# A four-layer hybrid trunk on one core: two-stream norms with their sums and products in PSUM, maps' slabs asked for two units ahead, the first norm's sums from the token tiles

## The chip, the cores and the metric

The kernel runs on one core of a Trainium2 chip, in one launch. The metric is the device time in microseconds (us). Three executions of the kernel before took 2185.64, 2183.06 and 2180.51 us, median 2183.06.

## The reference, cut to what matters

256 latent tokens (x) and 256 context tokens (ctx) of width 1024 go through four layers, in fp32: Hyena (long convolution), GLA (gated linear attention), MLA (latent attention), Hyena. Each layer has a mixer and an MLP, and ahead of both stands a norm that is modulated by six maps of the layer:

```python
mod_l = jnp.split((silu_c @ ada_w[i] + ada_b[i])[:, None, :], 6, axis=-1)      # ada_w[i]: 1024 x 6144
h_lat = modulate(rmsnorm(x_lat, norm1_g[i]), mod_l[0], mod_l[1])               # h * (1 + scale) + shift
x_lat = x_lat + mod_l[2] * mixer(h_lat)
x_lat = x_lat + mod_l[5] * sq_relu_mlp(modulate(rmsnorm(x_lat, norm2_g[i]), mod_l[3], mod_l[4]), w1, w2)
```

`rmsnorm` is y * rsqrt(mean(y*y) + 1e-6) * g. The context tokens take the same path with their own maps as long as a later layer reads them. So the norms of Hyena 0, its MLP, GLA, its MLP and MLA run on both streams (512 tokens); those of MLA's MLP and of layer 3 on the latent tokens alone.

## The kernel before, in words

The residual lies transposed: `xT[k]` (L324) holds features k*128 to k*128+127 of all 512 tokens, latent first. Every fp32 product is made of three fp32r matmuls (`mm3`, L368): both factors are split into a high part (fp32r) and the rest. Weights come as 512 KB slabs by SyncE's DMA queue (`wload`, L336); ScalarE (ACT) casts the high part `wh` (L359) and GpSimd (POOL) subtracts it for the low part `wl` (L360). There are 5 buffers of `wraw` and 4 each of `wh` and `wl`.

PSUM has eight banks, shared out by tag (L145): `mm` 2, `cv` 3, `ada` 1, `st` 2. `bank(tag)` (L149) takes one.

**The two-stream norm** (`norm_mod`, L515) runs `stream(0)` for the latent and `stream(1)` for the context tokens. For each stream `token_rstd` (L481) squares the eight feature tiles on ACT (L490; POOL in the very first norm, L488), adds them on VectorE (DVE) in SBUF (`sacc`, L497), sums over partitions on TensorE (PE) with ones (L501), and `rsqrt` (L470) makes exp(-0.5*ln(v)) on ACT (L474, L475) with one Newton step on DVE (L476 to L478). `token_diag` (L507) puts the result on a diagonal, on DVE (L510), and one matmul (L524) spreads it over the partitions as `rb`. Then, for each k:

```python
nc.vector.scalar_tensor_tensor(t, xT[k][:, s], sc, rb[:, :SEQ], ALU.mult, ALU.mult)      # L528, t in SBUF
nc.scalar.activation(uH[k][:, s], t, AF.Identity, bias=sh)                               # L529
nc.vector.scalar_tensor_tensor(uL[k][:, s], t, sh, rounded(uH[k][:, s]), ALU.add, ALU.subtract)   # L530
```

`stream(0)` is moved ahead of the second half of the residual product before it (`last_part`, L532). The first products behind a norm read the streams one after the other, so that they can start on the latent half. Behind an MLP's norm (`first_product`, L697) products 0 and 1 lie in `mm`, 2 and 3 in `cv`; behind Hyena 0's norm all three are in `mm` (L944); in GLA the gates' product is in `mm` (L175) and q and k of the first head in `cv` (L1193); MLA's q part is in `mm` (L1400), its key and value part in `cv` and `st`. The residual product before is in the other tag: mixers' in `mm`, MLPs' in `cv` (L646, L780).

**The one-stream norm** (`lone_norm`, L574) does the same for the latent tokens alone, behind its products; what it squares and splits (`fresh`) lies in PSUM, two features to a bank (L587, L588), and so does its running sum (L597). It shares `rsqrt` and `token_diag` (L610).

**The maps.** For layers 0 and 1, `ada_units` (L396) is a generator: one unit asks for one slab of `ada_w` (`adaw`, 3 buffers) and multiplies it on PE (L410). `pump(n, keep)` (L459) runs n units at set places: 16 up front, 8 among the filters, then 8 in step 0 and 4 in every other step of Hyena 0 (L1135), where `keep` 8 holds back the last map. Layer 1's units follow behind. The maps of layers 2 and 3 are made in GLA's MLP by `ada_lone` (L417): 96 units, each one slab (`lw`), summed on DVE (L434 to L442) in `st` banks; two of the maps need both streams. `more` (L758) lets a unit go each time that `total`/96 matmul counts have passed; `total` (L756) is 7*192-24 = 1320 for the MLP's eight groups.

The order on each engine is a planner's: instructions come in program order by priority, an engine takes the next one that is ready in the planner's own timing, and a tile waits for a free buffer of its tag. Tokens come in as eight tiles `xr` (L250), which PE transposes (L328) and DVE copies (L329). The start also makes the Hyena filters' input (L297 to L322).

Of the kernel before, what the change touches and what calls it, by code (L numbers as in the profile page):

```python
# [11 lines left out]
F32 = mybir.dt.float32  # L12
# [6 lines left out]
P = 128  # L19
# [108 lines left out]
def trunk_kernel(ctx: ExitStack, tc: tile.TileContext, ins: dict, table, zpos, out, layers=(0, 1, 2, 3)):  # L128
# [195 lines left out]
    xT = [cp.tile([P, TOK], F32, tag=f"x{k}", name=f"x{k}") for k in range(KD)]  # L324
    for k in range(KD):
        ps = bank("cv")
        for j in range(4):
            nc.tensor.transpose(ps[:, j * P : (j + 1) * P], xr[2 * j + k // 4][:, (k % 4) * P : (k % 4 + 1) * P], ident)  # L328
        nc.vector.tensor_copy(xT[k], ps)  # L329
# [38 lines left out]
    def mm3(ps, lh, ll, rh, rl, start, stop):  # L368
        nc.tensor.matmul(ps, lh, rh, start=start, stop=False)  # L369
        nc.tensor.matmul(ps, lh, rl, start=False, stop=False)  # L370
        nc.tensor.matmul(ps, ll, rh, start=False, stop=stop)  # L371
# [24 lines left out]
    def ada_units(i, parts, first=False):  # L396


        for q in parts:
            ps = bank("ada")  # L400
            for k in range(KD):
                tag, bufs = "adaw", 3
                if first and q < 2:
                    tag = (("adaw", "wraw", "wh", "wl") * 3 + ("wraw", "wh", "wl", "wraw"))[8 * q + k]
                    bufs = {"adaw": 3, "wraw": 5, "wh": 4, "wl": 4}[tag]
                wt = wp.tile([P, D], F32, tag=tag, name=nm("adaw"), bufs=bufs)
                nc.sync.dma_start(wt, g["ada_w"][i, k * P : (k + 1) * P, q * D : (q + 1) * D])
                wv = wt.rearrange("p (t j c) -> p j t c", j=4, c=32)
                for j in range(4):
                    nc.tensor.matmul(ps[32 * j : 32 * j + 32, :256], sT[:, k, :], wv[:, j],  # L410
                                     start=k == 0, stop=k == KD - 1, tile_position=(0, 32 * j))
                if k < KD - 1:
                    yield
            ada_part(i, q, ps[:, :256], slice(0, 2))
            yield
# [54 lines left out]
    def rsqrt(v, n):  # L470
# [5 lines left out]
        nc.vector.scalar_tensor_tensor(t, y, -0.5, y, ALU.mult, ALU.mult)  # L476
# [4 lines left out]
    def token_rstd(r, on_pool=False):  # L481

        s = slice(r * SEQ, (r + 1) * SEQ)
        acc = np_.tile([P, SEQ], F32, tag="sacc", name=nm("sacc"), bufs=1)

        def square(dst, k):
            if on_pool:
                nc.gpsimd.tensor_tensor(dst, xT[k][:, s], xT[k][:, s], ALU.mult)  # L488
            else:
                nc.scalar.activation(dst, xT[k][:, s], AF.Square)  # L490

        square(acc, 0)
        for k in range(1, KD):
            sq = np_.tile([P, SEQ], F32, tag="sq", name=nm("sq"))
            square(sq, k)
            if k < KD - 1:
                nc.vector.tensor_tensor(acc, acc, sq, ALU.add)  # L497
        ps = bank("st")
        for j in range(2):
            for e, a in enumerate((acc, sq)):  # L500
                nc.tensor.matmul(ps[:, 2 * j : 2 * j + 2], a[:, j * P : (j + 1) * P], ones[:, 0:2],  # L501
                                 start=e == 0, stop=e == 1)
        v = np_.tile([P, 2], F32, tag="rs_v", name=nm("rsv"))
        nc.vector.tensor_scalar(v, ps[:, 0:4:2], 1.0 / D, EPS, ALU.mult, ALU.add)
        return rsqrt(v, 2)
# [9 lines left out]
    def norm_mod(i, which, nt, first=False):  # L515
# [3 lines left out]
        uL = [up.tile([P, TOK], F32R, tag=f"uL{k}", name=nm("uL")) for k in range(KD)]  # L519
        def stream(r):  # L520
            s = slice(r * SEQ, (r + 1) * SEQ)
            y = token_rstd(r, first)
            rb = bank("st")
            nc.tensor.matmul(rb[:, :SEQ], ones, token_diag(y), start=True, stop=True)  # L524
            for k in range(KD):
                t = np_.tile([P, SEQ], F32, tag="xr", name=nm("xr"))
                sc, sh = a[:, which, k, r : r + 1], m[:, 3 * which, k, r : r + 1]
                nc.vector.scalar_tensor_tensor(t, xT[k][:, s], sc, rb[:, :SEQ], ALU.mult, ALU.mult)  # L528
# [45 lines left out]
    def lone_norm(i, which, mp):  # L574
# [27 lines left out]
        def statistics():  # L602
            ps = bank("st")
            for j in range(2):
                for e, a in enumerate((acc, sq)):
                    nc.tensor.matmul(ps[:, 2 * j : 2 * j + 2], a[:, j * P : (j + 1) * P], ones[:, 0:2],  # L606
                                     start=e == 0, stop=e == 1)
            v = np_.tile([P, 2], F32, tag="rs_v", name=nm("rsv"))
            nc.vector.tensor_scalar(v, ps[:, 0:4:2], 1.0 / D, EPS, ALU.mult, ALU.add)
            diag = token_diag(rsqrt(v, 2))  # L610
# [72 lines left out]
    def mlp(i, nt, later=None, lone=()):  # L683
        single = nt == SEQ
        if not single:
            u = norm_mod(i, 1, nt)
        with ExitStack() as es:
# [68 lines left out]
            total, count = (groups - 1) * (4 * 24 + 8 * 12) - 24, [0]  # L756
# [156 lines left out]
    def hyena(i, j, nt, build):  # L913

        two = nt == TOK
        if two:
            u = norm_mod(i, 0, nt, build)
# [4 lines left out]
        with tc.tile_pool(name=nm("hy"), bufs=2, reuse_waits="tile") as mp:  # L922
# [77 lines left out]
            with tc.tile_pool(name=nm("hc"), bufs=2, reuse_waits="tile") as mq:  # L1000
# [111 lines left out]
                for step in range(units + 1):  # L1112
# [22 lines left out]
                    pump(8 if step == 0 else 4, 8)  # L1135
# [18 lines left out]
    def gla(i, j):  # L1154
# [4 lines left out]
        u = norm_mod(i, 0, nt)  # L1159
# [212 lines left out]
    def mla(i, j):  # L1372
        nt = TOK
        QR, KVR = 384, 256
        u = norm_mod(i, 0, nt)
# [263 lines left out]
    y = token_rstd(0)  # L1639
# [39 lines left out]
```

## Time and profile before

| | |
|---|---|
| the profiled execution | 2186.09 us, its span 2184.3 us |
| median of three executions | 2183.06 us (2180.51 to 2185.64) |
| PE busy | 2071.4 us (95%) |
| DVE, ACT, POOL busy | 1276.7, 908.8, 1088.7 us |
| mean granted PE clock | 0.97 of 2.4 GHz |
| DMA | 329 MB, mean 151 GB/s |

Times in the views are us from the span's start. PE is busy almost throughout, so what a part of the kernel can give or take shows where PE stands idle or where its granted clock falls to the lower of its two levels (1.2 GHz, 0.5 of full speed). The other engines' busy shares say little: they work beside PE.

### The profile page before, as it was taken

What the parts mean: (1) busy time and instruction counts of PE and PEld (TensorE: products, weight loads), DVE (VectorE), ACT (ScalarE), POOL (GpSimd) and SP (SyncE); (2) the same over time, 40 slices, a digit from 0 to 9 for tenths busy, and PEclk for the clock granted to TensorE, in tenths of its full rate; (3) what the DMA queues carried; (4) which work ended last, traced back from release to release, by engine and by line L of the source; (5) the groups of instructions that cost most, each with busy time, mean ns of one, the idle gap of its engine ahead of it and who ended that gap; (6) DMA issues with size and microseconds to landing.
All of it is one profiled execution on the core that took longest, in us unless ns stands there. A gap on an engine that the chain in (4) does not pass through costs nothing. (4 is left out here: it accounts for less than half of the span.)

```text
span 2184.3 us, 33342 instructions
## 1 busy us (share of the span) xinstructions
PE 2071.4 (95%) x12882; PEld 1769.6 (81%) x12882; DVE 1276.7 (58%) x2378; ACT 908.8 (42%) x1529; POOL 1088.7 (50%) x637
## 2 busy tenths in 40 slices
PE   6998999889999999999989999998999998899998
PEld 3766687677888888887788778788789998888998
DVE  7864887765433335555466986677662224883323
ACT  2643343343333334555242223226454546554544
POOL 5663454346545433333134444434346887455885
PEclk7999999999999999999999999999999999999999
DMA  9676635533333332322127688753135665443663
GB/s 317 192 223 202 231 96 180 191 93 118 105 98 108 109 92 68 85 59 77 39 78 231 209 281 269 252 183 98 65 96 161 188 193 160 141 140 116 187 181 116
DMA packets 322301, 329.12 MB, mean 151 GB/s; under 512 B 21276, under 2 KB 248673, under 8 KB 322143
## 3 DMA queue, kind: packets, MB, share of 16 engines
q1 hardware_dynamic: 321012, 326.05, 48.1%
q8 instruction: 101, 1.65, 0.3%
q10 hardware_dynamic: 587, 0.61, 0.1%
q0 software_dynamic: 544, 0.34, 0.1%
q14 instruction: 57, 0.47, 0.1%
HBM read 317.51 MB, written 9.44 MB: 150 GB/s over the span
## 5 line engine op out<-in xcount | busy, mean ns | idle before, releaser
L360 POOL TENSOR_TENSOR wl<-wraw,wh 128x1024 fp32r<-128x1024 f32 (+2 forms) x378 | 908.5, 2418 | 894.0 <-ACT wh L359 838.9
L359 ACT CAST wh<-wraw 128x1024 fp32r<-128x1024 f32 (+2 forms) x378 | 390.7, 1042 | 624.6 <-PE mm L370 243.4
L369 PE MATMUL mm<-uH,wh 128*128 128x512 f32 (+3 forms) x1272 | 448.5, 356 | 18.2 <-ACT uH L587 6.7
L370 PE MATMUL mm<-uL,wh 128*128 128x512 f32 (+3 forms) x1272 | 449.7, 355 | 10.3 <-DVE uL L530 9.3
L371 PE MATMUL mm<-uH,wl 128*128 128x512 f32 (+3 forms) x1272 | 445.1, 352 | 0.0
L369 PEld LDWEIGHTS mm<-uH,wh 128*128 128x128 f32 (+1 forms) x1272 | 244.7, 194 | 62.4 <-issue 10.0
L370 PEld LDWEIGHTS mm<-uL,wh 128*128 128x128 f32 (+1 forms) x1272 | 246.2, 194 | 46.3 <-DVE uL L530 13.3
L371 PEld LDWEIGHTS mm<-uH,wl 128*128 128x128 f32 (+1 forms) x1272 | 246.7, 194 | 32.3 <-issue 3.8
L369 PE MATMUL cv<-fH,wh 128*128 128x512 f32 (+1 forms) x576 | 209.3, 369 | 7.1 <-ACT fH L176 6.0
L370 PE MATMUL cv<-fL,wh 128*128 128x512 f32 (+1 forms) x576 | 210.7, 367 | 0.7 <-DVE fL L177 0.6
L371 PE MATMUL cv<-fH,wl 128*128 128x512 f32 (+1 forms) x576 | 209.2, 366 | 0.0
L666 DVE SCALAR_TENSOR_TENSOR x<-cv,mods,x 128x256 f32<-128x256 f32 x256 | 112.3, 477 | 84.9 <-PE cv L371 84.9
L370 PE MATMUL sum<-fL,wh 128*128 128x256 f32 x512 | 138.8, 278 | 0.0
L369 PE MATMUL sum<-fH,wh 128*128 128x256 f32 x512 | 137.1, 278 | 0.0
L371 PE MATMUL sum<-fH,wl 128*128 128x256 f32 x512 | 136.7, 278 | 0.0
L369 PEld LDWEIGHTS cv<-fH,wh 128*128 128x128 f32 x576 | 108.1, 189 | 29.3 <-ACT fH L176 7.6
L370 PEld LDWEIGHTS cv<-fL,wh 128*128 128x128 f32 x576 | 108.6, 189 | 19.1 <-DVE fL L177 1.1
L718 DVE SCALAR_TENSOR_TENSOR mm<-mm,r 128x512 f32<-128x512 f32 x60 | 41.8, 696 | 139.1 <-ACT r L717 138.9
L371 PEld LDWEIGHTS cv<-fH,wl 128*128 128x128 f32 x576 | 108.6, 189 | 17.7 <-issue 0.2
L436 DVE SCALAR_TENSOR_TENSOR st<-lw,sT,st 128x512 f32<-128x512 f32 x144 | 101.2, 747 | 8.3 <-DMA lw<-in_ada_w_dram 8.2
L621 DVE COPY rbias<-st 128x1 f32<-128x1 f32 x32 | 5.1, 159 | 163.1 <-PE st L371 162.9
L370 PEld LDWEIGHTS sum<-fL,wh 128*128 128x128 f32 x512 | 95.2, 188 | 0.0
(526 smaller groups left out, 4498.1 us busy)
## 6 DMA issues: line engine op xcount, KB each, us to landing
wraw<-in_mlp_w_dram SPq DMA_DIRECT2D x256, 512.0 KB
adaw<-in_ada_w_dram SPq DMA_DIRECT2D x96, 512.0 KB
lw<-in_ada_w_dram SPq DMA_DIRECT2D x96, 512.0 KB
wraw<-in_hy_w_in_dram SPq DMA_DIRECT2D x48, 512.0 KB
wraw<-in_gla_w_in_dram SPq DMA_DIRECT2D x24, 512.0 KB
spec<-S SPq DMA_DIRECT2D x16, 512.0 KB
wraw<-in_hy_w_out_dram SPq DMA_DIRECT2D x16, 512.0 KB
S<-spec SPq DMA_DIRECT2D x32, 256.0 KB
```

Of the source, the lines that this page charges most:

```text
L359: nc.scalar.copy(wh[r0:r1, :n], raw[r0:r1, :n])
L360: nc.gpsimd.tensor_tensor(wl[r0:r1, :n], raw[r0:r1, :n], rounded(wh[r0:r1, :n]), ALU.subtract)
L369: nc.tensor.matmul(ps, lh, rh, start=start, stop=False)
L370: nc.tensor.matmul(ps, lh, rl, start=False, stop=False)
L371: nc.tensor.matmul(ps, ll, rh, start=False, stop=stop)
L436: nc.vector.scalar_tensor_tensor(dst, wt[:, cols], sT[:, k, 0:1], run[b], ALU.mult, ALU.add)
L621: nc.vector.tensor_copy(bias, ps[:, SEQ : SEQ + 1])
L666: add = nc.vector.scalar_tensor_tensor(xT[dt][:, q], ps[:, q], mods[i][:, gi, dt, r : r + 1], xT[dt][:, q], ALU.mult, ALU.add)
L718: nc.vector.scalar_tensor_tensor(r, r, 0.0, pos, ALU.max, ALU.mult)
```

## The change

- The first norm's mean squares come from the token tiles: eight ACT squares with an accumulated sum, for both streams, ahead of the transposes; half of the transposes' copies go to ACT. The POOL squares, the `sacc` sums and the L501 matmuls of that norm fall away.
- In all two-stream norms one `st` bank holds the running sum, the four token sums, two operands of `rsqrt` and then `rb`; `t` goes to PSUM, two features to a bank, in `mm` (mixers) or `cv` (MLPs). `rsqrt` gets one more Exp, into PSUM, and `token_diag` moves to ACT. The one-stream norms take over these last two.
- `ada_units` asks for the slab of unit n+2 in unit n, from the same three buffers. `pump` in Hyena 0 gives 4 units in step 0 and 2 in the others.
- `total` becomes 6*192 = 1152.

```diff
+    def transpose_in(k):
+        ps = bank("cv")
+        for j in range(4):
+            nc.tensor.transpose(ps[:, j * P : (j + 1) * P], xr[2 * j + k // 4][:, (k % 4) * P : (k % 4 + 1) * P], ident)
+        (nc.scalar.copy if k % 2 else nc.vector.tensor_copy)(xT[k], ps)
...
+    sums = cp.tile([P, 8], F32, tag="xsum", name="xsum")
+    junk = wp.tile([P, SLOT], F32, tag="wl", name="junk", bufs=4)
+    for b in range(8):
+        nc.scalar.activation(junk[:, :512], xr[b], AF.Square, accum_out=sums[:, b : b + 1])
+    means = cp.tile([P, 4], F32, tag="xmean", name="xmean")
+    nc.vector.tensor_tensor(means, sums[:, 0:8:2], sums[:, 1:8:2], ALU.add)
+    nc.vector.tensor_scalar(means, means, 1.0 / D, EPS, ALU.mult, ALU.add)
     for k in range(KD):
...
+        transpose_in(k)
...
     def ada_units(i, parts, first=False):
...
+        slabs = [(q, k) for q in parts for k in range(KD)]
+        loaded = {}
+
+        def load(n):
+            q, k = slabs[n]
+            tag, bufs = "adaw", 3
...
+            loaded[n] = wp.tile([P, D], F32, tag=tag, name=nm("adaw"), bufs=bufs)
+            nc.sync.dma_start(loaded[n], g["ada_w"][i, k * P : (k + 1) * P, q * D : (q + 1) * D])
+
+        for n, (q, k) in enumerate(slabs):
+
+            for ahead in range(n, min(n + 3, len(slabs))):
+                if ahead not in loaded:
+                    load(ahead)
+            if k == 0:
+                ps = bank("ada")
+            wv = loaded.pop(n).rearrange("p (t j c) -> p j t c", j=4, c=32)
+            for j in range(4):
+                nc.tensor.matmul(ps[32 * j : 32 * j + 32, :256], sT[:, k, :], wv[:, j],
+                                 start=k == 0, stop=k == KD - 1, tile_position=(0, 32 * j))
...
-    def rsqrt(v, n):
+    def rsqrt(v, n, ps=None):
...
         nc.scalar.activation(y, t, AF.Exp, scale=-0.5)
-        nc.vector.scalar_tensor_tensor(t, y, -0.5, y, ALU.mult, ALU.mult)
+        y2 = y
+        if ps is not None:
+            y2 = ps[:, :n]
+            nc.scalar.activation(y2, t, AF.Exp, scale=-0.5)
+            t = ps[:, n : 2 * n]
+        nc.vector.scalar_tensor_tensor(t, y2, -0.5, y, ALU.mult, ALU.mult)
...
-    def token_rstd(r, on_pool=False):
+    def token_rstd(r, ps):
...
+        run = ps[:, :SEQ]
         acc = np_.tile([P, SEQ], F32, tag="sacc", name=nm("sacc"), bufs=1)
...
+        for k in range(KD):
+            sq = np_.tile([P, SEQ], F32, tag="sq", name=nm("sq")) if k else None
+            nc.scalar.activation(sq if k else run, xT[k][:, s], AF.Square)
+            if 0 < k < KD - 1:
+                nc.vector.tensor_tensor(acc if k == KD - 2 else run, run, sq, ALU.add)
+        st = ps[:, SEQ : SEQ + 4]
...
+        return rsqrt(v, 2, ps[:, SEQ + 4 : SEQ + 8])
...
         for j in range(2):
-            nc.vector.tensor_scalar(diag[:, j], ident, y[:, j : j + 1], None, ALU.mult)
+            nc.scalar.activation(diag[:, j], ident, AF.Copy, scale=y[:, j : j + 1])
...
-    def norm_mod(i, which, nt, first=False):
+    def norm_mod(i, which, nt, tag, known=None):
...
-            y = token_rstd(r, first)
-            rb = bank("st")
-            nc.tensor.matmul(rb[:, :SEQ], ones, token_diag(y), start=True, stop=True)
+            ps = bank("st")
+            y = token_rstd(r, ps) if known is None else known[:, 2 * r : 2 * r + 2]
+            rb = ps[:, :SEQ]
+            nc.tensor.matmul(rb, ones, token_diag(y), start=True, stop=True)
             for k in range(KD):
-                t = np_.tile([P, SEQ], F32, tag="xr", name=nm("xr"))
+                if k % 2 == 0:
+                    t2 = bank(tag)
+                t = t2[:, k % 2 * SEQ : (k % 2 + 1) * SEQ]
...
-            total, count = (groups - 1) * (4 * 24 + 8 * 12) - 24, [0]
+            total, count = (groups - 2) * (4 * 24 + 8 * 12), [0]
...
-            u = norm_mod(i, 0, nt, build)
+            u = norm_mod(i, 0, nt, "mm", rsqrt(means, 4) if build else None)
...
-                    pump(8 if step == 0 else 4, 8)
+                    pump(4 if step == 0 else 2, 8)
```

The other calls pass `"mm"` (GLA, MLA) and `"cv"` (MLP); `statistics` in `lone_norm` (L602) passes four columns of its `st` bank to `rsqrt`, and the final norm a bank of its own.

## Rows read from the trace of the kernel before

**Rows 1.** The profile page: busy us, share of the span and instructions of the engines.

```profile
PE 2071.4 (95%) x12882; PEld 1769.6 (81%) x12882; DVE 1276.7 (58%) x2378; ACT 908.8 (42%) x1529; POOL 1088.7 (50%) x637
```

**Rows 2.** Windows: start:end and length, busy us by engine, granted clock, DMA share, GB/s.

```profile
36.00:60.00 24.00, 19.08 (x89) 12.85 (x82) 21.83 (x34) 11.72 (x21) 16.23 (x12) 0.57 1.03 303
175.00:195.00 20.00, 14.40 (x107) 8.90 (x97) 6.08 (x15) 4.05 (x7) 2.41 (x1) 0.74 0.88 298
400.00:412.00 12.00, 10.01 (x86) 6.88 (x85) 7.66 (x11) 3.19 (x5) 5.63 (x5) 0.86 0.83 299
428.00:460.00 32.00, 26.36 (x179) 23.55 (x179) 27.19 (x52) 14.26 (x31) 10.58 (x8) 0.95 0.26 78
833.00:848.00 15.00, 11.59 (x66) 10.41 (x65) 12.97 (x30) 7.70 (x17) 7.06 (x5) 0.77 0.49 137
1099.00:1118.00 19.00, 12.98 (x70) 12.31 (x69) 14.49 (x27) 7.24 (x15) 5.91 (x3) 0.73 0.33 110
1199.00:1264.00 65.00, 62.60 (x283) 49.65 (x282) 63.13 (x88) 15.38 (x19) 28.24 (x11) 0.97 0.68 212
1485.00:1500.00 15.00, 12.55 (x54) 11.02 (x54) 14.71 (x27) 8.61 (x18) 8.81 (x4) 0.77 0.46 131
```

**Rows 3.** PE's waits: what it waited for, us in total, times, longest.

```profile
PE ada L410 <- DMA adaw<-in_ada_w_dram: 11.3, 12, 2.9
PE mm L370 <- DVE uL L530: 9.3, 8, 2.1
PE st L501 <- DVE sacc L497: 5.5, 4, 2.9
```

**Rows 4.** Timeline of all engines from 1102.4 us: start, duration, instruction, idle before it.

```profile
1102.85 4.84 POOL L360 TENSOR_TENSOR wl<-wraw,wh 128x1024 fp32r<-128x1024 f32 x2 [2.79 <-ACT wh L359]
1103.12 2.37 DVE L497 TENSOR_TENSOR sacc<-sacc,sq 128x256 f32<-128x256 f32 x1
...
1105.42 2.56 DVE L530 SCALAR_TENSOR_TENSOR uL<-xr,mods,uH 128x256 fp32r<-128x256 f32 x1
1105.64 0.35 PE L501 MATMUL st<-ones,sacc 128*128 128x2 f32 x2 [1.48 <-DVE sacc L497]
...
1108.03 0.58 PE L370 MATMUL mm<-uL,wh 128*128 128x256 f32 x1 [2.03 <-DVE uL L530]
```

**Rows 5.** Single lines: duration in ns min/median/max, first and last start.

```profile
L530 DVE SCALAR_TENSOR_TENSOR uL<-xr,mods,uH x80: 466/484/3711, 40.1 to 1511.8; 128x256 fp32r<-128x256 f32 x80
...
L588 DVE SCALAR_TENSOR_TENSOR uL<-sum,adam,uH x24: 473/476/484, 1630.3 to 1987.6; 128x256 fp32r<-128x256 f32 x24
...
L497 DVE TENSOR_TENSOR sacc<-sacc,sq x66: 405/424/2372, 16.9 to 2175.5; 128x256 f32<-128x256 f32 x66
...
L597 DVE TENSOR_TENSOR mm<-mm,sq x15: 417/431/433, 1633.4 to 1988.7; 128x256 f32<-128x256 f32 x15
...
L528 DVE SCALAR_TENSOR_TENSOR xr<-x,adam,st x80: 461/473/482, 39.0 to 1509.8; 128x256 f32<-128x256 f32 x80
```

**Rows 6.** Single lines, the same columns: ACT's shares of a norm.

```profile
L475 ACT ACTIVATE rsy<-rst x20: 190/204/207, 31.5 to 2177.6; 128x2 f32<-128x2 f32 x15, 128x4 f32<-128x4 f32 x5
...
L587 ACT ACTIVATE uH<-sum,adam x24: 464/476/556, 1629.6 to 1987.0; 128x256 fp32r<-128x256 f32 x24
```

**Rows 7.** MLA's norm, timeline of all engines: its first product and its second.

```profile
1484.27 0.87 DVE L528 SCALAR_TENSOR_TENSOR xr<-x,adam,st 128x256 f32<-128x256 f32 x2
...
1485.34 0.44 PE L369 MATMUL mm<-wh,uH 128*128 128x384 f32 x1
...
1494.54 0.73 PE L369 MATMUL cv<-wh,uH 128*128 128x320 f32 x2
```

**Rows 8.** First norm, timeline of PE: the wait for the second sum, and the first product.

```profile
39.27 0.56 PE L501 MATMUL st<-ones,sacc 128*128 128x2 f32 x2 [2.92 <-DVE sacc L497]
...
45.05 0.58 PE L369 MATMUL mm<-uH,wh 128*128 128x256 f32 x1
```

**Rows 9.** What ACT's L587 waited for in the one-stream norms: us, times.

```profile
  DVE uL L588: 1.4, 4
```

More of the change, by code (lines that the diff above doesn't have):

```diff
@@ L324, in trunk_kernel @@
     xT = [cp.tile([P, TOK], F32, tag=f"x{k}", name=f"x{k}") for k in range(KD)]
+    sums = cp.tile([P, 8], F32, tag="xsum", name="xsum")
[5 more added lines that the diff above has]
+    nc.vector.tensor_scalar(means, means, 1.0 / D, EPS, ALU.mult, ALU.add)
     for k in range(KD):
[L326 to L329, printed above, removed]
+        transpose_in(k)
     pre = nc.scalar.preload_act_table_set("natural_log_exp_and_others")
@@ L370, in mm3 @@
         nc.tensor.matmul(ps, lh, rl, start=False, stop=False)
-        nc.tensor.matmul(ps, ll, rh, start=False, stop=stop)
+        return nc.tensor.matmul(ps, ll, rh, start=False, stop=stop)
     mods = {}
@@ L396, in ada_units @@
     def ada_units(i, parts, first=False):
[L399 to L414, printed above, removed]
+        slabs = [(q, k) for q in parts for k in range(KD)]
[3 more added lines that the diff above has]
+            tag, bufs = "adaw", 3
+            if first and q < 2:
+                tag = (("adaw", "wraw", "wh", "wl") * 3 + ("wraw", "wh", "wl", "wraw"))[8 * q + k]
+                bufs = {"adaw": 3, "wraw": 5, "wh": 4, "wl": 4}[tag]
+            loaded[n] = wp.tile([P, D], F32, tag=tag, name=nm("adaw"), bufs=bufs)
[10 more added lines that the diff above has]
+                                 start=k == 0, stop=k == KD - 1, tile_position=(0, 32 * j))
+            if k == KD - 1:
+                ada_part(i, q, ps[:, :256], slice(0, 2))
+            loaded[n] = None
             yield
@@ L479, in rsqrt @@
         return y
-    def token_rstd(r, on_pool=False):
+    def token_rstd(r, ps):
         s = slice(r * SEQ, (r + 1) * SEQ)
+        run = ps[:, :SEQ]
         acc = np_.tile([P, SEQ], F32, tag="sacc", name=nm("sacc"), bufs=1)
[L486 to L498, printed above, removed]
+        for k in range(KD):
[4 more added lines that the diff above has]
+        st = ps[:, SEQ : SEQ + 4]
         for j in range(2):
             for e, a in enumerate((acc, sq)):
-                nc.tensor.matmul(ps[:, 2 * j : 2 * j + 2], a[:, j * P : (j + 1) * P], ones[:, 0:2],
+                nc.tensor.matmul(st[:, 2 * j : 2 * j + 2], a[:, j * P : (j + 1) * P], ones[:, 0:2],
                                  start=e == 0, stop=e == 1)
         v = np_.tile([P, 2], F32, tag="rs_v", name=nm("rsv"))
-        nc.vector.tensor_scalar(v, ps[:, 0:4:2], 1.0 / D, EPS, ALU.mult, ALU.add)
-        return rsqrt(v, 2)
+        nc.vector.tensor_scalar(v, st[:, 0:4:2], 1.0 / D, EPS, ALU.mult, ALU.add)
+        return rsqrt(v, 2, ps[:, SEQ + 4 : SEQ + 8])
     def token_diag(y):
@@ L603, in statistics @@
             ps = bank("st")
+            st = ps[:, SEQ : SEQ + 4]
             for j in range(2):
                 for e, a in enumerate((acc, sq)):
-                    nc.tensor.matmul(ps[:, 2 * j : 2 * j + 2], a[:, j * P : (j + 1) * P], ones[:, 0:2],
+                    nc.tensor.matmul(st[:, 2 * j : 2 * j + 2], a[:, j * P : (j + 1) * P], ones[:, 0:2],
                                      start=e == 0, stop=e == 1)
             v = np_.tile([P, 2], F32, tag="rs_v", name=nm("rsv"))
-            nc.vector.tensor_scalar(v, ps[:, 0:4:2], 1.0 / D, EPS, ALU.mult, ALU.add)
-            diag = token_diag(rsqrt(v, 2))
+            nc.vector.tensor_scalar(v, st[:, 0:4:2], 1.0 / D, EPS, ALU.mult, ALU.add)
+            diag = token_diag(rsqrt(v, 2, ps[:, SEQ + 4 : SEQ + 8]))
             def rstd():
@@ L1638, in trunk_kernel @@
         transposed(k)
-    y = token_rstd(0)
+    y = token_rstd(0, bank("st"))
     transposed(KD - 1)
```

8 lines of the change are left out of this document (4 added, 4 removed).

## The prediction

> **What bounds the kernel now.** The page comes first: PE is busy 2071 of 2184 us [rows 1], so only some 113 us of idle time, and what the lower clock costs, can be won without taking work from PE. The change takes almost none from it. Next the waits of PE: for slabs of the maps 11.3 us, for `uL` of a two-stream norm 9.3 us, for the sum of squares 5.5 us [rows 3]. All three sit where the change edits. Third the windows around these waits, which show where, and the clock with it: a mean granted clock of 0.73 over 19 us means that (1 - 0.73) * 19 = 5.1 us of PE work were lost at the lower level. Idle time and this loss together are what a window can give back at most [rows 2].
>
> Last the timeline inside one norm, for the cause. Both DVE instructions that PE waits for run into a pair of POOL subtractions: a `sacc` addition that began at 1103.12, behind a POOL start at 1102.85, took 2.37 us, and the `uL` after it 2.56 us, ending about when POOL did [rows 4]. Undisturbed they take 0.42 and 0.48 us. Over the run the SBUF-only L530 reaches 3.7 us and L497 2.4 us, while the same operations with one operand in PSUM, L588 and L597, never pass 0.484 and 0.433 us, though POOL is as busy there [rows 5]. So these two are slow where both tensor inputs lie in SBUF and POOL is at work. The change puts one of them into PSUM.
>
> **The sum, part by part.** The profiled execution took 2186.09 us, 1.8 over its span and 3.0 over the median; the sum is made against it, and 3.0 is taken off at the end.
>
> *MLP norms (428 to 460, 1099 to 1118).* Idle 32 - 26.4 = 5.6 and 19 - 13.0 = 6.0 us, clock loss 1.6 and 5.1: 18.4 us to give [rows 2]. `t` in `cv` doesn't collide with the residual product before it, in `mm`; products 0 and 1 have `mm`. But products 2 and 3 want `cv` too, so PE may have two or three products to alternate between in place of four, and DVE makes a feature only every 0.473 + 0.484 us [rows 5]. Ends +4 and +18; I take two thirds, **+12**, because the waits named in the list go whole.
>
> *GLA's and MLA's norms (833 to 848, 1485 to 1500).* Idle 3.4 and 2.5, clock loss 3.4 and 3.4: 12.8 us to give [rows 2]. Against it: `t` in `mm` holds both banks, and MLA's first product wants `mm` as well. The norm's first tile starts at 1484.27 and PE at 1485.34 [rows 7]. A bank is back when six features are through, 6 * 0.957 = 5.7 us after the start: PE would wait 4.7 us where it waits 2.5 now. Key and value parts, in `cv`, come no earlier than 1494.5 today. GLA's q and k lie in `cv` and can run meanwhile. Ends +12.8 and -15 (below, first rival); I take GLA +4, MLA -2: **+2**.
>
> *First norm (36 to 60).* Idle 4.9 us, clock loss 10.3 [rows 2], 2.9 of it the wait for the second stream's sum [rows 8], which goes since both sums are known early. Eight squares and four copies more on ACT fall into the first 20 us, where it does little. But all three first products are in `mm`, beside sixteen features' tiles, and the DMA share of the window is 1.03: slabs and weights cannot come faster. If both streams' tiles go first, fourteen features must pass, 39.0 + 14 * 0.957 = 52.4, against a first product at 45.05 now [rows 5, 8]. Ends +15 and -7; nearest is the wait that surely goes, with some clock: **+5**.
>
> *Slabs ahead, fewer units at a time.* 175 to 195 loses 5.6 us idle and 5.2 of clock, 400 to 412 2.0 and 1.7 [rows 2]: 14.5. The waits of PE for slabs in the whole run are 11.3 us in 12 pieces [rows 3], those of the start among them. In these windows the DMA share is 0.88 and 0.83: a burst of units outruns the loads. With 4 and 2 units to a step the first two of a burst have their slabs already. There are still three buffers, so a request two ahead waits in SP's queue for the unit before, and weights behind it wait too; PE's weights came in time so far, and no wait for them is in the list of any size. Ends 0 and +15; **+9**, because DVE, ACT and POOL idle in 175 to 195 too, so that PE's place in its queue alone holds everything up.
>
> *Late maps.* 96 units over 1152 counts in place of 1320, so one per 12 in place of 13.75. Where two streams are summed DVE is busy 63.1 of 65 us [rows 2]; that stretch would shrink to 65 * 12 / 13.75 = 56.7 us. DVE falls 6.4 us behind if nothing else in it shrinks, less as its main work does; the main evictions queue behind it and PE waits for banks, as it does in that window now (2.4 us). Ends -9 (6.4 and clock) and +1; **-4**.
>
> *Newton step and diagonal.* One Exp more per stream, 0.2 us on ACT [rows 6], and the diagonal moves from DVE to ACT at about the same length. Where PE waits for it (one-stream and last norms, four times) that is -1, and up to +2 if stalls go: **0**.
>
> Sum: 12 + 2 + 5 + 9 - 4 = 24 us. 2186 - 24 = 2162, less 3.0: **2159 us**.
>
> **Rivals.**
>
> *Banks for products (slower).* The norm's tiles of both streams go before the products in `mm`. For: both streams precede them in program order. Against: the second stream's tiles wait for their own sums, and a product may slip in. Price: MLA waits for fourteen features, 1484.3 + 13.4 = 1497.7, so 12.3 us in place of 2.5, with 1.7 more of clock (5.1 as after 6.0 us of idle [rows 2]): -12; GLA's gates and half of its v wait, -3; the first norm -7. 12 - 12 - 3 - 7 + 9 - 4 = -5: **2188 us** by the median. It decides once bank waits in these three norms pass 17 us.
>
> *Turns in a bank.* Two features share a bank, so ACT reading one and DVE writing the other may have to take turns. In the one-stream norms, which lie like this already, ACT waited for DVE four times in 24, 1.4 us in all [rows 9], so I give it nothing in the sum. A pair that is made fully in turns takes 2 * (0.473 + 0.476 + 0.476) = 2.85 us in place of 1.91 [rows 5, 6], 3.8 us per stream of eight features; in the four later norms, with the second stream hidden behind the first's products, 15 us: **2174 us**. The Trainium skill, page "PSUM — Partial Sum Buffer", section "PSUM bank collisions raise a hardware error", speaks against the change here: any two engines on one bank and quadrant at once collide, two readers included, and must be ordered by bank. By that rule alone turns are certain and only two banks in rotation hide them; rows 9 show the turns, and that they are short.
>
> *Requests are not earlier.* With three buffers the planner asked as early before as it can now; only the smaller pumps remain, and other fillers take their place in bursts. For: SP asked for three slabs in a row already. Against: the bursts themselves are thinner. The slabs' +9 goes: **2168 us**.
>
> *DVE bounds the late maps.* All 9 us and a second drop of the clock, some 12 in place of 4: **2167 us**. For: 97% busy there. Against: the mean over the MLP is far lower, and the backlog drains.
>
> **How the numbers follow.** About 0.2% (4.4 us) is what a measurement of this kernel can tell from no change, so faster is below 2178.7 and slower above 2187.4. Chances: forecast 0.52, banks 0.13, turns 0.13, requests 0.14, DVE 0.08. Of the forecast's 0.52 nearly all is faster (0.50; 0.02 same); of turns 0.09 and 0.04, of requests 0.12 and 0.02, of DVE 0.07 and 0.01; of banks 0.12 slower and 0.01 same. Together faster 0.78, same 0.10, slower 0.12. The range: the ends of the five terms are independent, and some 15 us each way hold the forecast's own case (2144 to 2174); turns, requests and DVE reach it to about 2181 with their own spread, and all norms at their upper ends to 2140. Outside lie the banks (0.12) and some 0.06 besides.
>
> **What would show it.** Right: L530 and L497 with a maximum near 0.5 us in norms behind the first; PE's waits for `uL` and for the sum under 5 us together in place of 14.8, for slabs under 5 in place of 11.3; granted clock over 0.9 in the windows of both MLP norms and of 175 to 195. In the late maps DVE near 100% over some 57 us with PE waits of 4 to 6 us. Wrong: first products in `mm` starting over 5 us after the residual product in MLA, or after 50 us in the first norm (banks); ACT and DVE alternating without overlap in a norm (turns); SP's requests for slabs as late, with PE waiting 10 us for them (requests). The sum is wrong altogether if PE's idle time falls by over 20 us and the time does not, or the reverse.

## The result, and the profile after

The changed kernel takes 2242.22 us (median of four runs, 2235.87 to 2248.60); the ratio to the kernel before is 1.0252, 95% interval 1.0228 to 1.0276. That is 55 us slower, where 24 us faster was forecast. A ratio of 0.001 is 2.2 us in what follows.

The engines' busy times of the changed kernel, to be read against [rows 1]:

```profile
PE 2086.1 (93%) x12866; PEld 1778.9 (79%) x12866; DVE 1219.5 (54%) x2333; ACT 1007.4 (45%) x1652; POOL 1076.9 (48%) x621
```

The span is 2239.4 us, 55.1 longer. PE's work has hardly changed, but it is busy 14.7 us more (its mean granted clock is 0.958, before 0.97) and idle 40.4 us more. DVE does 57 us less, partly because work went to ACT. ACT does 99 us more in 123 instructions more. Eight squares and four copies of 0.6 us, short exponentials and diagonals cannot be 99 us, so ACT's groups come next (line, engine, operation, count, busy us and mean ns, share of the span):

```profile
L495 ACT ACT_TABLE_LOAD x18 | 23.1, 1283 | 0.3
L494 ACT ACT_TABLE_LOAD x18 | 23.1, 1283 | 0.3
L1176 ACT ACT_TABLE_LOAD x14 | 18.0, 1283 | 0.2
L1243 ACT ACT_TABLE_LOAD x7 | 9.0, 1283 | 0.1
L1266 ACT ACT_TABLE_LOAD x4 | 5.1, 1283 | 0.1
```

With six more groups these are 69 loads of ACT's function tables (`ACT_TABLE_LOAD`), 88.5 us in all. The kernel before has two: one at its start, and the preload of the set that holds both log and exp (L331):

```profile
L180 ACT ACT_TABLE_LOAD x1 | 1.3, 1283 | 0.7 <-PEq L1664 0.7
L331 ACT ACT_TABLE_LOAD x1 | 1.3, 1283 | 0.0
```

The loads of the changed kernel stand on the log and the exp of `rsqrt` (L494, L495) and on those of GLA's gates and decays (L1176, L1243, L1266), lines that the change left as they were. Where it begins is seen in ACT's timeline at the start of the changed kernel:

```profile
18.00 0.58 ACT L257 COPY x<-cv 128x512 f32<-128x512 f32 x1 [0.29 <-PE cv L256]
18.60 1.28 ACT L341 ACT_TABLE_LOAD   x1
19.89 0.20 ACT L494 ACTIVATE rst<-xmean 128x4 f32<-128x4 f32 x1
20.12 1.28 ACT L301 ACT_TABLE_LOAD   x1
21.41 0.42 ACT L301 ACTIVATE scr<-scr 128x256 f32<-128x256 f32 x1
21.84 1.28 ACT L495 ACT_TABLE_LOAD   x1
```

The preload (L341) runs at 18.6 us, behind a copy and ahead of a sine of the filters (L301). The sine needs another set and puts it in; from there nearly every log and every exp of `rsqrt` has a load of its own (18 loads on the 19 calls of each). `keep_in_program_order` (the line behind the preload) pins it to the instruction of ACT that stands just ahead of it in the program. Before, that was the copy behind the last sine (L321):

```profile
29.23 0.76 ACT L321 CAST h<-scr 64x256 fp32r<-64x256 f32 x2
30.00 1.28 ACT L331 ACT_TABLE_LOAD   x1
```

The change put half of the transposes' copies on ACT between the two (L257), and so moved the pin from the sines to a copy that starts 11 us earlier (18.00 against 29.23 us).

In GLA these loads lie on the path of PE. ACT in the changed kernel, second head:

```profile
926.21 0.63 ACT L1175 ACTIVATE gl<-gl 128x512 f32<-128x512 f32 x1
926.86 1.28 ACT L1176 ACT_TABLE_LOAD   x1
928.16 0.63 ACT L1176 ACTIVATE sg<-sg 128x512 f32<-128x512 f32 x1
...
929.81 1.28 ACT L1243 ACT_TABLE_LOAD   x1
931.11 0.63 ACT L1243 ACTIVATE sg<-sg 128x512 f32<-128x512 f32 x1
931.64 0.61 ACT L1175 ACTIVATE gl<-gl 128x512 f32<-128x512 f32 x1
932.27 1.28 ACT L1176 ACT_TABLE_LOAD   x1
```

DVE waits longer for the gates (between 868 and 1106 us 27.9 us for L1176's `sg`; 18.9 in run e1 below, which has no such loads), and the longest waits of PE in the changed kernel now include GLA's (`sf` belongs to its scan, `diag` to MLA's norm):

```profile
PE cv L1302 <- DVE sf L1294: 6.7, 2, 5.5
...
PE st L546 <- ACT diag L529: 5.4, 1, 5.4
...
PE st L1291 <- DVE sf L1277: 4.3, 3, 2.3
```

Counting the first matmul of each of `mm3`'s triples as one product, from zero, the changed kernel is 0.7 us ahead in front of GLA's attention (1280th product, 926.98 against 927.63 us) and 29.7 us behind at its end (1480th, 1117.74 against 1088.02). The Trainium skill, page "ScalarE: Activation LUTs", section "What ACT_TABLE_LOAD costs", gives 1283 ns for the load, as the rows do, and some 1380 ns to drain the engine, which they don't show: from the start of one activation to that of the next are 1.95 us over a load (926.21 to 928.16) and 0.53 without one (931.11 to 931.64), so a load costs 1.4.

What was to be won is there. Both forms of `uL` of the changed kernel, against a maximum of 3711 ns in [rows 5]:

```profile
L554 DVE SCALAR_TENSOR_TENSOR uL<-mm,mods,uH x48: 466/478/485, 38.7 to 1529.6; 128x256 fp32r<-128x256 f32 x48
L554 DVE SCALAR_TENSOR_TENSOR uL<-cv,mods,uH x32: 468/478/486, 436.8 to 1148.6; 128x256 fp32r<-128x256 f32 x32
```

And in MLA the banks' wait that a rival described (DVE's first feature, PE's diagonal of the second stream, its first product, in the changed kernel):

```profile
1508.40 0.48 DVE L552 SCALAR_TENSOR_TENSOR mm<-x,adam,st 128x256 f32<-128x256 f32 x1
```

```profile
1519.87 1.22 PE L546 MATMUL st<-diag,ones 128*128 128x256 f32 x2 [5.38 <-ACT diag L529]
1528.24 0.69 PE L379 MATMUL mm<-wh,uH 128*128 128x384 f32 x1 [7.14 <-DVE uL L554]
```

19.8 us from feature to product, where [rows 7] show 1.1; in e1, without the loads, it is 17.2 (1485.49 to 1502.71).

### The profile page after: what moved, and what is told of

The parts are those of the page before. It is cut to its first block, busy times and chain, and to the rows that moved or that the text cites. A ratio compares the mean times of both kernels' runs of the same rounds, so it can differ in the third digit from the quotient of the medians.

```text
span 2239.4 us, 33367 instructions
## 1 busy us (share of the span) xinstructions
PE 2086.1 (93%) x12866; PEld 1778.9 (79%) x12866; DVE 1219.5 (54%) x2333; ACT 1007.4 (45%) x1652; POOL 1076.9 (48%) x621
## 5 line engine op out<-in xcount | busy, mean ns | idle before, releaser
L380 PEld LDWEIGHTS cv<-fL,wh 128*128 128x128 f32 x576 | 109.1, 189 | 18.6 <-issue 0.7
L379 PEld LDWEIGHTS sum<-fH,wh 128*128 128x128 f32 x512 | 95.0, 188 | 0.0
```

## The experiments

**The loads.** e1 is the changed kernel with the preload queued behind the sines again; e2 is the kernel before with the one line that moves the pin.

```diff
-            nc.scalar.copy(dst[:fw], hv[:fw])
+            chain_end = nc.scalar.copy(dst[:fw], hv[:fw])
...
-    pre = nc.scalar.preload_act_table_set("natural_log_exp_and_others")
+    with tc.issue_after(chain_end.ins):
+        pre = nc.scalar.preload_act_table_set("natural_log_exp_and_others")
```

> The changed kernel with one edit: the preload of ACT's set with both log and exp (L341) is queued behind the last copy that follows the filters' sines, as it stood in the kernel before. Theory 'tables': in the changed kernel the preload ran at 18.6 us, ahead of two sines, the sine replaced the set, and from then on every log and every exp loads a set of its own, 69 loads of 1.28 us in place of 2. Then this kernel shows 2 or 3 loads, PE's wait in GLA between the second and the last quarter goes (30 us of the 52), the norms behind it give some 10 more: 2242 falls to 2195 us (2180 to 2210). Rival 'banks': the loss is that norms hold the banks of the products (forecast 2188 for that) and the order of GLA that follows from it; the loads lie on ACT, which is busy 45% and hides them: no less than 2232 us. Both theories together: what is left above 2184 is the banks' share, at least 12 us of it in MLA's norm, where the first product starts over 15 us after the norm's first tile.

```diff
-        nc.vector.tensor_copy(xT[k], ps)
+        (nc.scalar.copy if k % 2 else nc.vector.tensor_copy)(xT[k], ps)
```

> The kernel before with one line of the change: every second copy behind the transposes of the tokens is ACT's in place of DVE's. These four copies take 0.6 us each beside idle time. Theory 'tables': they are traced between the sines and the preload, the preload is pinned to the last of them instead of to the sines' copies, runs ahead of a sine, and the log and exp of all four layers load sets again: over 50 loads, and 2215 us (2200 to 2230), most of the 30 us in GLA. Rival 'nothing but copies': 2184 us within 4.

e1: 2193.41 us, ratio to the kernel before 1.0036 (95% interval 1.0022 to 1.0050). e2: 2244.95 us, 1.0286 (1.0265 to 1.0308). All loads of e1, and the first of e2's eleven groups (71 loads):

```profile
L180 ACT ACT_TABLE_LOAD x1 | 1.3, 1283 | 0.7 <-PEq L1690 0.7
L342 ACT ACT_TABLE_LOAD x1 | 1.3, 1283 | 0.0
```

```profile
L474 ACT ACT_TABLE_LOAD x20 | 25.7, 1283 | 0.4
L475 ACT ACT_TABLE_LOAD x19 | 24.4, 1283 | 0.3
L1151 ACT ACT_TABLE_LOAD x14 | 18.0, 1283 | 0.2
```

The loads cost 1.0252 - 1.0036 = 0.0216, 47 us, and four copies of 0.6 us alone bring them on and cost 62 us (of which some 12 may be the copies' own price, by e12 against e11 below). In GLA's attention e1 loses nothing (1280th to 1480th product: 160.3 us, before 160.4). The two windows over GLA, changed kernel and e1 (PE, PEld, DVE, ACT, POOL busy, clock, DMA):

```profile
868.00:1106.00 238.00, 210.30 (x1092) 172.12 (x1090) 110.34 (x172) 152.32 (x251) 67.98 (x27) 0.94 0.21 62
```

```profile
868.00:1106.00 238.00, 229.19 (x1319) 194.70 (x1317) 125.03 (x207) 118.94 (x244) 78.19 (x33) 0.98 0.24 69
```

ACT is busy only 64% of the window in the slow one. That ACT is "busy 45% and hides them" was the rival's argument in e1's expectation, and it is wrong: the loads stand in a chain from ACT to DVE to PE.

**What holds e1 at 1.0036.** Four undoings, each of one part, on e1. e3 has `total` 1320 again; e4 the units and pumps of before; e5 and e6 have `t` in SBUF again in MLA's and in the first norm (of e4 the pumps' line alone is shown):

```diff
-            total, count = (groups - 2) * (4 * 24 + 8 * 12), [0]
+            total, count = (groups - 1) * (4 * 24 + 8 * 12) - 24, [0]
```

> All from here start from e1 (2193.4 us), in which the loads of sets are gone. Here `total` is 1320 again, so one late map's unit per 13.75 counts in place of 12. Theory 'DVE bounds the late maps': e1 lost 8 us against the kernel before between its 1234 and 1304 us, where DVE is busy 53 of 55 us and PE waits 5.8 us for a residual on DVE; with the wider spacing these 8 us come back: 2185.5 us (2182 to 2189), and the 5.8 us wait is gone. Rival 'another order, not the spacing': 2193 within 3.

```diff
-                    pump(4 if step == 0 else 2, 8)
+                    pump(8 if step == 0 else 4, 8)
```

> e1 with the maps' units and the pumps of the kernel before: no request ahead, 8 and 4 units to a step. In e1 PE waits 25.5 us for slabs, before 11.3; the longest wait (7.0 us, at 46 us) stands in the first norm. Theory 'requests ahead cost': a request two ahead stands in SP's queue ahead of the weights, slabs and weights share a queue whose engines are busy over 100%, so PE waits for both: 2184 us (2180 to 2189). Rival 'it was to help, and helps elsewhere': e1 is nearly even with the kernel before from 60 to 400 us because the smaller pumps save what the start loses: 2196 us or more. Rival 'only moved': 2193 within 3, and PE's waits for slabs stay above 20 us because the start has too little else to do.

```diff
-                if k % 2 == 0:
-                    t2 = bank(tag)
-                t = t2[:, k % 2 * SEQ : (k % 2 + 1) * SEQ]
+                t = np_.tile([P, SEQ], F32, tag="xr", name=nm("xr"))
```

> e1 with the features of MLA's norm in SBUF again, sums and the rest still in PSUM. Theory 'banks': both streams' features hold the two banks of `mm` ahead of the first product, which starts 16 us after the norm's first tile in e1 and 1.1 us after it before; that costs 11 us: 2183 us (2179 to 2187), first product within 3 us of the first feature. Rival 'the second stream's sum': PE waits for the diagonal of the second stream, which stands ahead of the product in PE's queue, and it does so with SBUF too: 2190 us or more.

> e1 with the features of the first norm in SBUF, its mean squares still from the token tiles. In e1 the first product starts at 62.8 us (45.05 before) and PE is busy 6.7 us between 40 and 60 us (18.0 before). Theory 'banks' (sixteen features hold both banks of `mm`): first product at 45 to 48 us, PE busy over 13 us in that window, and the time falls by about half of what is lost there, since later work fills PE anyway: 2188 us (2183 to 2192). Rival 'slabs and weights bound the start' (DMA share 1.14): the product starts earlier but the time stays 2193 within 3.

| | ratio | interval | against e1 |
|---|---|---|---|
| e3 late maps | 1.0004 | 0.9991 to 1.0018 | -7.0 us |
| e4 units and pumps | 1.0032 | 1.0016 to 1.0049 | -0.9 us |
| e5 MLA's features | 0.9981 | 0.9967 to 0.9995 | -12 us |
| e6 first norm's features | 1.0060 | 1.0042 to 1.0079 | +5.2 us |

e3 and e5 came out near what their theories had. e6 lies above e1, but their intervals overlap. The late maps, e1 and then e3, same window:

```profile
1195.00:1260.00 65.00, 59.23 (x272) 46.26 (x271) 59.85 (x91) 14.08 (x19) 28.79 (x10) 0.95 0.69 220
```

```profile
1195.00:1260.00 65.00, 63.01 (x291) 49.81 (x290) 64.05 (x90) 15.67 (x19) 29.63 (x12) 1.00 0.70 221
```

In 65 us PE got 3.8 us more done, and DVE 4.2. The waits of DVE in e1 in this window, and of PE in it and a little further:

```profile
DVE st L457 <- DMA lw<-in_ada_w_dram: 5.0, 4, 3.1
```

```profile
PE cv L380 <- DVE x L692: 5.8, 1, 5.8
PE cv L380 <- ACT fH L176: 2.0, 1, 2.0
```

The 5.8 us are all of PE's idle time in e1's window: it waits, until 1243.69, for a residual that stands behind the maps' additions in DVE's queue (1.7 us in e3). In the stretch in which PE stands, DVE is busy 5.4 of 6 us, and its longest wait for a slab comes only behind it:

```profile
1238.00:1244.00 6.00, 0.31 (x1) 0.34 (x2) 5.43 (x9) 0.58 (x1) 0.00 (x0) 0.71 0.63 195
```

```profile
1256.76 1.42 DVE L457 SCALAR_TENSOR_TENSOR st<-lw,sT,st 128x512 f32<-128x512 f32 x2 [3.08 <-DMA lw<-in_ada_w_dram]
```

Of DVE's waits for slabs 1.9 us lie ahead of that residual (1.1, 0.2 and 0.6). So late slabs can explain at most a third of PE's wait; the rest is DVE's own work on the maps in front of the residuals, as the forecast had it, at a higher price. In e5 MLA's first product starts at 1481.48, 2.3 us behind the first feature at 1479.17; the rival, that the second stream's diagonal stands in the way in any case, falls.

e4 came out as its rival "only moved": PE still waits 20.0 us for slabs. e6 missed. Its first product did start at 44.23 in place of 62.81, and at the 120th product it was 13.6 us ahead of e1, but at the 200th 6.5 us behind. e1 and e6 early, then e6 where it lost it:

```profile
40.00:60.00 20.00, 6.68 (x34) 2.12 (x32) 17.43 (x26) 10.30 (x20) 15.16 (x10) 0.50 1.14 306
```

```profile
40.00:60.00 20.00, 13.68 (x67) 9.88 (x68) 18.27 (x26) 9.55 (x17) 15.16 (x9) 0.71 1.13 302
...
160.00:180.00 20.00, 14.59 (x117) 9.54 (x119) 6.50 (x14) 5.61 (x8) 8.40 (x7) 0.91 0.76 262
180.00:200.00 20.00, 14.77 (x90) 10.28 (x90) 6.61 (x15) 3.03 (x5) 0.00 (x0) 0.66 0.72 257
```

From 160 to 200 us all engines idle and the DMA is not full: PE stands in its queue before units whose slabs have not landed (7.6 of its 10.6 us of idle time). What the start wins is waited for there.

**Both at once, and all four.** e7 and e8 tried whether e4's and e6's losses hide each other (e7 undoes both, e8 keeps the request ahead); e9 undoes all that had a price (units, pumps and `total` as before, the features of the first and of MLA's norm in SBUF); e10 is e9 with these features in `cv` and asks whether only the tag was wrong.

> e6 (features of the first norm in SBUF, ratio to the kernel before 1.0060) with the units and pumps of the kernel before as well. e6 was 13.6 us ahead of e1 at its 120th product and 6.5 us behind at its 200th: between 160 and 200 us PE stood still for slabs while POOL had nothing to do, SP's queue held slabs for units two ahead, which wait for one of three buffers. e4, with units of before, lost nothing there. Theory 'two losses that hide each other': each undone alone gives nothing, both together give what e6 had gained by 120 us, 10 to 14 us: ratio 0.9995 (0.997 to 1.0015). Rival 'the start and the filters are bound by the DMA queue, whatever the order': 1.003 or more, like e4.

> The same with the pumps of before but the request two ahead kept. If the request ahead is what costs (slabs wait in SP's queue for a buffer with weights behind them): like e6, 1.005 or more. If the thinner pumps cost (units heap up and all stand at one place): like e7, 0.9995 within 0.002.

> e1 with all that has cost something undone: units, pumps and total of the kernel before, features of the first and of MLA's norm in SBUF. What stays of the change: first sums from the token tiles, sums of the norms and operands of the root in PSUM, features in PSUM in GLA's and in the MLPs' norms, diagonal on ACT. Theory 'parts add': e1 1.0036, less 0.0032 (late maps), 0.0055 (MLA) and 0.004 (first norm with units): 0.991 (0.988 to 0.994), some 2166 us where the kernel before takes 2185: the gain forecast for the MLPs' norms, 8 us, with 3 in GLA and 5 in the one-stream norms. Rival 'gains depend on each other': 0.996 or more.

> e9 with the features of the first and of MLA's norm in `cv` in place of SBUF, so that they don't hold the banks of the first product. Theory 'only the tag was wrong': as good as e9 or up to 4 us better, because those features are then free of POOL: ratio 0.989 (0.986 to 0.992), MLA's first product within 3 us of the first feature. Rival 'any bank collides': `cv` holds the MLP's residual ahead of MLA, its key part behind, and the filters at the start; 5 us or more worse than e9.

e7: 1.0045 (1.0029 to 1.0062) and e8: 1.0039 (1.0025 to 1.0052): no. The pumps and the request ahead are worth nothing that these runs tell apart, and the theory of two hidden losses fell. e9: 0.9943 (0.9929 to 0.9957), 2173.39 us, a gain, though short of 0.991. e10: 0.9986 (0.9972 to 1.0001): the features of both norms in `cv` are 9 us worse than in SBUF, the rival's price. But this is not MLA's. There the first product comes 2.3 us behind the first feature, as in SBUF:

```profile
1478.97 0.49 DVE L543 SCALAR_TENSOR_TENSOR cv<-x,adam,st 128x256 f32<-128x256 f32 x1
```

```profile
1481.28 0.34 PE L380 MATMUL mm<-wh,uH 128*128 128x384 f32 x1
```

From the 2040th to the 2120th product e10 takes 38.3 us, e9 36.8 and e1, with the features in `mm`, 50.9. So for MLA "only the tag was wrong" came near, and "any bank collides" can hold for the first norm alone: at the 480th product e10's trace is 10.0 us behind e9's. e9 loses against the kernel before only up to Hyena 0's end (7.6 us behind at the 480th product) and gains 22 us from there to its last product.

**The start.** e11 is e9 with the first norm wholly as before, e12 adds the copies on ACT (with the preload in its place), e13 is the kernel before with `t` in PSUM in GLA's and the MLPs' norms and nothing else, e14 is e11 with the diagonal on DVE, e15 undoes only e3's and e5's parts, e16 is e14 with the new first norm, e17 is e1 with the diagonal on DVE:

```diff
-            nc.scalar.activation(diag[:, j], ident, AF.Copy, scale=y[:, j : j + 1])
+            nc.vector.tensor_scalar(diag[:, j], ident, y[:, j : j + 1], None, ALU.mult)
```

> e9 with the first norm wholly as before: squares and sums on POOL and DVE, no squares of the token tiles, all copies behind the transposes on DVE. What stays of the change: GLA's and the MLPs' features in PSUM, the later norms' running sums and root in PSUM, the diagonal on ACT. e9 runs 4.8 us ahead of the kernel before at its 160th product and 7.6 us behind at its 480th, though its units are those of before; from there to the end it gains 22 us. Theory 'the new first norm has put the slabs and weights of the first 240 us in another order, at a loss': the 7.6 us come back, 0.9943 becomes 0.991 (0.989 to 0.993), some 2165 us where the kernel before takes 2185, the 18 to 22 us that were forecast for the norms alone. Rival 'it is the later norms, or the diagonal on ACT, that reach back into the order of Hyena 0': 0.9943 within 0.0012.

> e11 and every second copy behind the transposes on ACT, with the preload behind the sines. If the copies are what reorders the start, as e2 hints (7.1 us behind the kernel before at its 240th product, where only five of its loads had run): like e9, 0.994 or more. If the sums from the token tiles do it: like e11 within 0.001.

> The kernel before with one part of the change alone: the features t of GLA's and the MLPs' norms in PSUM, two to a bank. Everything ahead of the first MLP is as before. Forecast of these terms: 12 + 4 us; e1 showed 1.6 + 2.8 + 6.1 = 10.5 us in these three norms with the sums in PSUM too. Theory 'the features carry the norms' gain': 0.9955 (0.993 to 0.998). If the lag of Hyena 0 comes from the first norm, the diagonal or the copies: 480th product within 3 us of the kernel before. If it comes with any change (the later norms reach back): 5 us or more behind there.

> e11 (0.9922) with the diagonal on DVE as before. If the diagonal on ACT is what puts Hyena 0 in another order: the 480th product within 3 us of the kernel before and 0.989 (0.987 to 0.991). If it is not: 0.9922 within 0.0015, and the 480th product still 6 us or more behind.

> e1 with the two parts undone that e3 and e5 priced (late maps 7 us, MLA's features 12 us), all else of the change kept, the new first norm and the requests ahead too. Theory 'parts add': 1.0036 - 0.0032 - 0.0055 = 0.9949 (0.993 to 0.997), level with e9, in which the start is as before in three more respects: then the start's parts are worth nothing either way. Rival: 0.998 or more, if e9's gain needed the old start.

> e14 (0.9871) with the new first norm: mean squares from the token tiles on ACT, half of the copies on ACT, features in SBUF; that is e9 (0.9943) with the diagonal on DVE. If the new first norm's gain (4.8 us ahead at e9's 160th product) stays once the diagonal is on DVE: 0.985 (0.983 to 0.987). If the copies and squares cost in the order of the start, as e12 against e11 hints (0.0055): 0.9925 (0.990 to 0.995).

> e1 (1.0036), the whole change with the preload behind the sines, with the diagonal on DVE. If the diagonal costs what it cost in e11 (0.005, 11 us): 0.9985 (0.9965 to 1.0005). If e1's start is lost to the banks of its first norm whatever the diagonal does: 1.0036 within 0.0015.

| | ratio | interval | 480th product (before 402.7 us) |
|---|---|---|---|
| e11 | 0.9922 | 0.9896 to 0.9948 | 412.3 |
| e12 | 0.9977 | 0.9962 to 0.9993 | 413.9 |
| e13 | 0.9988 | 0.9976 to 1.0000 | 407.2 |
| e14 | 0.9871 | 0.9850 to 0.9892 | 401.4 |
| e15 | 0.9958 | 0.9942 to 0.9975 | 409.9 |
| e16 | 0.9939 | 0.9925 to 0.9953 | 413.7 |
| e17 | 0.9999 | 0.9985 to 1.0012 | 408.5 |

The lag at the 480th product is read from one trace of each, and it needs care. Up to there e13 and e14 run PE's instructions, and ask for slabs and weights on SP's queue, in the same order as the kernel before, and still lie 5.8 us apart.

e11's ratio lies inside what its theory had, but its interval holds the rival's 0.9943 too, and with the old first norm the lag stayed. e14 shows what made it there, the diagonal on ACT. The wait itself is small, in e11 and then e14:

```profile
34.04 1.22 PE L560 MATMUL st<-diag,ones 128*128 128x256 f32 x2 [1.88 <-ACT diag L539]
```

```profile
33.27 0.98 PE L560 MATMUL st<-diag,ones 128*128 128x256 f32 x2 [0.65 <-DVE diag L539]
```

1.2 us at 34 us became 11 us at 400 us; 11 us (0.0051) is also what the runs give. e12 against e11 puts 0.0055, 12 us, on the four copies alone; e9, which is e12 with the sums from the token tiles, is 7 us better again. e16 shows that the new first norm does harm alone: it costs 0.0068, 15 us, against e14, while with it the diagonal's place no longer matters (e9 0.9943, e16 0.9939). In the whole change it does matter (e17 0.9999, e1 1.0036: 8 us). The stretch where it happens, e14 and then e16 (PE busy, clock, DMA share):

```profile
60.00:160.00 100.00, 96.94 (x596) 0.98 0.64 200
160.00:260.00 100.00, 87.09 (x616) 0.97 0.65 217
```

```profile
60.00:160.00 100.00, 99.71 (x624) 0.99 0.68 212
160.00:260.00 100.00, 83.07 (x536) 0.88 0.58 191
```

As in e6, e16 is faster up to 160 us and slower behind it. What these moves change, far from where they stand, is the order in which SP asks for slabs and weights. e11's order leaves e14's at the 63rd load, e12's leaves e11's and e16's leaves e14's at the 34th, e17's leaves e1's at the 65th; up to the 480th product e9's and e16's are one order, and their times agree. So the loads' order is the likely link, which no run tests by itself; by what rule the planner turns one place of the order into the other was not found. e15 is 0.0015 short of e9, with intervals that overlap, so the start's other parts are worth little once the loads, the late maps and MLA are out.

e14, 2162.47 us where the kernel before took 2188.46, is the fastest version: GLA's and the MLPs' features, the later norms' sums and the root in PSUM (the root in the one-stream norms too), and nothing else of the change. Its engines, and its waits of PE for slabs:

```profile
PE 2060.5 (95%) x12882; PEld 1761.4 (81%) x12882; DVE 1241.1 (57%) x2378; ACT 908.4 (42%) x1541; POOL 1086.8 (50%) x637
```

```profile
PE ada L414 <- DMA adaw<-in_ada_w_dram: 12.5, 13, 3.1
```

The slabs are asked for as before, and waited for as before (11.3 us in [rows 3]); what went is in the norms.

## Why the prediction was wrong

The step that failed is a sentence of the first norm's term: "Eight squares and four copies more on ACT fall into the first 20 us, where it does little". Their time was put at nothing, and what they stand in front of was not asked. The preload behind them is pinned to its neighbour in the program, and the copies became that neighbour. What the runs showed in its place: 69 loads instead of 2, and 47 us (1.0252 against e1's 1.0036). This was in the diff and in the code, not in the trace; no rival had it, and it is larger than the whole range, 41 us. The rival on the other side, "banks", had the right sign and MLA's price, but nothing of the loads.

- **Norms in PSUM.** `L530 and L497 with a maximum near 0.5 us`: right (486 ns; the sums' additions 433 ns in e1). The forecast of 12 for the MLPs and 4 for GLA: e14 gains 2.6 us from the 480th to the 720th product (the first MLP's norm), 2.6 to the 1480th (GLA), 8.5 to the 1680th (the second MLP's norm), 1.9 to the 2040th (the late maps) and 5.4 to the 2120th (MLA's norm, whose features lie in SBUF). So the sum of the first and third, 11.1, is near the 12. The features alone (e13) missed their 0.9955 with 0.9988, 2.6 us in the whole run; in the same five stretches e13's trace gains 2.9, -1.6, 3.2, 2.1 and 0.1 us (the 2.1, in the late maps, where e13 changes nothing, shows how far one trace can be trusted). So the features bring about half of the MLPs' gain and none that can be told in GLA; what e14 has more would come with the sums and the root in PSUM, which no run has alone.
- **MLA's and the first norm's banks.** Term -2, and rival -12: MLA measured 12.0 us (e5). The forecast took one stream's six features ahead of the product; both streams' came, as the rival said, and the product came 17.2 us behind the first feature (e1), 19.8 with the loads. In another tag, `cv`, the features hold nothing up there (e10). In the first norm they came too (first product at 62.81 us in e1), where the later slab waits took the 18 us back, so that it cost nothing that can be told.
- **First norm, +5.** Wrong in sign: -15 us (e16 against e14, features in SBUF), with the loads apart; with the diagonal on ACT -5, which the intervals do not tell from nothing (e9 against e11): -12 for the copies on ACT (e12 against e11) and +7 for the sums from the token tiles (e9 against e12). These sums without the copies were not run.
- **Slabs ahead, +9.** Nothing that can be told: undone, the time falls by 0.9 us (e4) and 3.3 (e7 against e6), within the intervals. The 9 go, as the rival "requests are not earlier" had it; PE's waits for slabs did not fall (14.7 us in the changed kernel, 11.3 before).
- **Late maps, -4.** -7.0 (e3), inside the ends -9 and +1: the mechanism was right in the main (the residual behind DVE's additions), the size too small, and late slabs have a part in it.
- **Newton and diagonal, 0, -1 to +2.** The diagonal on ACT cost 8 us in the whole change (e1 against e17) and 11 in e11 (against e14). Its direct wait, 1.2 us, lay at the range's lower end; what followed from it in the order did not.
- **Turns in a bank.** Not tested by itself, but e1's trace shows the pace: in the second MLP's norm a pair of features takes 1.94 us (two begin at 1116.35 us, the next two at 1118.29), and in MLA's as well (1490.39 to 1492.33), where the rival had 2.85 and the forecast 1.91. So banks in rotation hide whatever turns there are.
- **Clock in the windows.** The forecast's clock loss counts PE's idle time too: while PE was busy it is 4.7 and not 5.1 us from 1099 to 1118 us, and 3.7 and not 5.2 from 175 to 195. No term changes its sign by this.

Put together, 24 forecast and -55 measured, 79 us apart: the loads take 47, the first norm 20 (-15 for +5), MLA's banks 10 (-12 for -2), the slabs 9, the diagonal 8, the late maps 3, and the later norms with their sums give 12 more than their terms (e14's 28 for 16). That makes 85; the parts overlap: the first norm and the diagonal together are 16 us (e9 against e14), not 15 + 8, which leaves 78.

## What to carry to other kernels

Ask of every instruction that moves to another engine what is pinned to it or ahead of it there: a preload of a function set, pinned "behind what stands before", is a promise about program order, and an edit between the two breaks it without touching it. Look for table loads by name and count in any profile of ACT before reading waits. Features that wait in the banks of the product they feed hold that product until the last of them is through: count both streams, or give them another tag. And compare the order of the load queue before and after: the move of one short instruction changed it here from the 63rd load on.

## What was not expected of the hardware

Loads of 1.28 us on an engine that is 45% busy cost 47 us of the 86 that 67 of them take; 29 stand at GLA's gates and decays with DVE and PE behind, and there PE lost 30 us. The two-input DVE operations that POOL held up to 3.7 us are down to 0.486 with one operand in PSUM, in all 80 cases of e1: the Trainium skill, page "SBUF — State Buffer", section "Who interferes with whom", says that a DVE operation with two inputs in SBUF contends with a GpSimd instruction that reads SBUF, through a port that they share, and the trace agrees: in e14 the same line reaches 2.578 us where the features lie in SBUF and 0.486 where they lie in PSUM. A start that was 13.6 us faster (e6 against e1, at the 120th product) was paid back in full 80 products later, in a kernel that PE bounds at 95%.
